# Four conditioning chunks behind the layer branch, and two combinings behind the last activation

## The chip, the core and the metric

The kernel runs on one core of a Trainium2 chip. The metric is device time in microseconds (us), from the program's start to its end. The engines are TensorE (PE: matmuls; PEld: its weight loads), VectorE (DVE), ScalarE (ACT), GpSimd (POOL) and SyncE (SP), which here only issues transfers; 16 DMA engines move data. Matmul results go to PSUM, everything else on the chip lies in SBUF.

## What is computed

A two-layer network over 256 latent tokens and 256 context tokens, 1024 features wide, batch 1. Of the reference, what matters here:

```python
for l in range(DEPTH):                       # DEPTH = 2
    mod = jax.nn.silu(c) @ w_ada[l] + b_ada[l]          # 6 vectors of 1024
    mod_c = jax.nn.silu(c_ctx) @ w_ada[l] + b_ada[l]
    x, xc = trunk_layer(x, xc, mod, mod_c, ..., need_ctx_out=(l < DEPTH - 1))
return rms_norm(x, norm_f)

def trunk_layer(...):
    sh1, sc1, g1, sh2, sc2, g2 = jnp.split(mod[:, None, :], 6, axis=-1)
    x = x + g1 * token_mixer(modulate(rms_norm(x, norm1), sh1, sc1), ...)
    x = x + g2 * moe_ffn(modulate(rms_norm(x, norm2), sh2, sc2), ...)   # 16 experts, top 2 of one group
```

Conditioning vector number 3 of a layer is sh2, the shift ahead of the experts. The token mixer has two attentions, a Fourier and a pooling branch, each gated. An expert computes silu(x w1) * (x w3) and multiplies the product with w2.

## The kernel before, in words

**Products.** Weights are f32 in HBM. A chunk of 1 MB (128 x 2048 f32) is loaded to a stage buffer and split into two f16 tiles: ScalarE writes whi, VectorE the remainder wlo (lines 319 and 323, `split`). A product is then three f16 matmuls: whi x high, whi x low, wlo x high (L580 to L582, `mm3`). Conditioning chunks (kind "ada") and the w2 chunks of the last expert (WHOLE) are exceptions: they are "raw", multiplied in f32 straight from the stage buffer.

**The weight stream.** `Stream` holds the order of all chunks, found by a dry run of the same program. `get` takes the next chunk and lets `fill` issue loads on SP as far as buffers are free (four, NSTG, in the mixer). A buffer of a split chunk is free after its split, that of a raw chunk after its matmuls. `tick` asks for one more split ahead, within `look` chunks. The stream of layer 2 (`Wn`) is made and filled with its first four loads inside the last steps of layer 1 (`batch`), behind a VectorE memset.

**The branch.** Behind the experts of each layer stands a branch (`tc.If`, L1511) for a second round of experts that these inputs don't need. All engines meet there: none starts on layer 2 before the last one has come.

**Conditioning.** `ada(l, which)` makes one vector in four chunks: 8 x 2 f32 matmuls with 32 columns (L500) give sums in PSUM, `split` turns them into adah and adal, and `second` turns those into columns (L477, L478; small VectorE instructions L481, L488). It is a generator; in layer 2 `ada(1, 3)` is the list SIDE1 and is advanced by `with_side` at every third step of the filling work in the first attention. Its chunks stand in the weight stream where the dry run asks for them.

**Start of layer 2.** `norm_steps`: four diagonal tiles from the norms (L555), then per feature block k matmuls with x (L568) into one of four PSUM tiles "mm", ScalarE's h (L572), VectorE's hH and hL (L573, L574). `W.tick(ahead)` asks for the first splits before the blocks. `project` takes the keys' and values' chunk first.

**The end.** The last expert (e = 15) runs w1, then w3 (`up`), then `hidden`: ScalarE's Silu and VectorE's product sa (L1382, L1383), then `down` with raw w2 (L1312). Experts 0 to 13 have put their results in DRAM; these are gathered per token tile t and rank (POOL, L1399). `combine(t, True)` scales and adds the gathered rows: L1406 on ScalarE, L1407, L1409, L1410 on VectorE. Experts 14 and 15 reach the tokens through a matmul with the transposed one-hot matrix (`back`, L1333, tiles acc), whose results `add` joins to x (yl L1340, then L1345). yHL is the split of `down`'s result. The output is normed and stored.

**Order on the engines.** Tile's scheduler orders each engine's instructions by a model of their readiness. `keep_in_program_order` pins an instruction behind the one that was traced before it on the same engine; what is traced later may still be put ahead of either. An engine then takes its queue in that order.

## Time and profile before

| | |
|---|---|
| median of three runs | 1454.68 us (1453.69 to 1455.19) |
| the profiled execution's own time | 1449.04 us |
| its span, first to last instruction | 1447.30 us |
| mean granted TensorE clock | 0.984 of full |
| TensorE busy | 1345.9 us, 93% |
| VectorE busy | 1118.3 us, 77% |
| ScalarE busy | 952.8 us, 66% |
| DMA | 383.31 MB, mean 265 GB/s |

The profile is of one execution; its times count from the span's start. A busy TensorE is not TensorE at its peak, and a share over the whole span mixes stages with different limits. A wait is read with the engine and line that ended it.

### The profile page before, as it was taken

Reading aid. Unit: us, or ns where it says so; the run is one execution under the profiler, and the core shown is the slowest. Engines: PE = TensorE matmul, PEld = TensorE weight load, DVE = VectorE, ACT = ScalarE, POOL = GpSimd, SP = SyncE. Lnnn points to the kernel's source line nnn. Section 1 sums busy time; section 2 is a strip of 40 time slices with the busy share of each in tenths; the row PEclk is TensorE's granted clock in tenths of the full one; section 3 lists DMA queues with packets and bytes.
Section 4 is the critical chain, followed back from the end, with each engine's and each line's share of the span. In section 5 each row is a group of like instructions: output and inputs, shape, how many; then the busy total and the mean of one; then the engine's idle time right before and its main releaser. Section 6 shows DMA issues by size and latency. Waiting matters only on the chain. (4 is left out here: it accounts for less than half of the span.)

```text
span 1447.3 us, 33640 instructions
## 1 busy us (share of the span) xinstructions
PE 1345.9 (93%) x14151; PEld 923.4 (64%) x14151; DVE 1118.3 (77%) x2003; ACT 952.8 (66%) x1431; POOL 16.5 (1%) x16
## 2 busy tenths in 40 slices
PE   5999999999999998999999978899999989999994
PEld 3545445444444586777777746577788767777771
DVE  3888647786554557898988889878977888989995
ACT  3777535665433347889888656856855569899981
POOL 0000000000000000000000010000000000000010
PEclk9999999999999999999999999999999999999997
DMA  9559772678794336789999564783999679999981
GB/s 365 216 132 222 217 232 88 175 219 228 238 364 159 131 101 250 293 344 420 395 419 380 222 253 163 200 240 103 238 310 364 239 280 342 420 420 418 405 327 63
DMA packets 146416, 383.31 MB, mean 265 GB/s; under 512 B 91856, under 2 KB 93904, under 8 KB 108112
## 3 DMA queue, kind: packets, MB, share of 16 engines
q1 hardware_dynamic: 133136, 355.24, 69.5%
q10 hardware_dynamic: 11392, 19.56, 3.6%
q0 software_dynamic: 1728, 6.29, 1.3%
q8 instruction: 112, 1.84, 0.5%
q14 instruction: 48, 0.39, 0.1%
HBM read 344.88 MB, written 15.20 MB: 249 GB/s over the span
## 5 line engine op out<-in xcount | busy, mean ns | idle before, releaser
L323 DVE SCALAR_TENSOR_TENSOR wlo<-stage,whi 128x1024 f16<-128x1024 f32 (+1 forms) x212 | 318.5, 1522 | 104.0 <-ACT whi L319 103.6
L582 PE MATMUL mm<-hH,wlo 128*128 128x96 f16 (+2 forms) x1824 | 395.5, 260 | 1.0 <-DVE wlo L323 1.0
L580 PE MATMUL mm<-hH,whi 128*128 128x96 f16 (+2 forms) x1824 | 395.3, 260 | 0.7 <-DVE gate L992 0.7
L581 PE MATMUL mm<-hL,whi 128*128 128x96 f16 (+2 forms) x1824 | 395.3, 260 | 0.0
L319 ACT ACTIVATE whi<-stage 128x1024 f16<-128x1024 f32 (+1 forms) x212 | 269.6, 1294 | 126.3 <-PE mm L581 86.7
L582 PEld LDWEIGHTS <-wlo 128*128 128x128 f16 x3104 | 304.0, 98 | 72.7 <-DVE wlo L323 2.7
L580 PEld LDWEIGHTS <-whi 128*128 128x128 f16 x3104 | 303.9, 98 | 71.6 <-issue 3.4
L581 PEld LDWEIGHTS <-whi 128*128 128x128 f16 x3104 | 303.9, 98 | 71.2 <-issue 1.2
L323 DVE SCALAR_TENSOR_TENSOR wlo<-ext,whi 128x2048 f16<-128x2048 f32 x116 | 262.1, 2286 | 42.6 <-ACT whi L319 42.6
L319 ACT ACTIVATE whi<-ext 128x2048 f16<-128x2048 f32 x116 | 217.8, 1904 | 9.4 <-PE mm L582 7.4
L581 PE MATMUL mm<-xg,whi 128*128 128x96 f16 x1024 | 132.3, 206 | 0.0
L582 PE MATMUL mm<-xg,wlo 128*128 128x96 f16 x1024 | 132.3, 206 | 0.0
L580 PE MATMUL mm<-xg,whi 128*128 128x96 f16 x1024 | 132.3, 206 | 0.0
L581 PE MATMUL py<-wlo,hd 128*96 128x512 f16 x240 | 90.9, 379 | 8.9 <-DVE wlo L323 8.7
L582 PE MATMUL py<-whi,hd 128*96 128x512 f16 x240 | 90.2, 381 | 6.8 <-DVE hd L321 6.0
L580 PE MATMUL py<-whi,hd 128*96 128x512 f16 x240 | 91.0, 379 | 0.0
L580 PE MATMUL mm<-brH,whi 128*128 128x512 f16 (+1 forms) x256 | 83.5, 326 | 0.0
L582 PE MATMUL mm<-brH,wlo 128*128 128x512 f16 (+1 forms) x256 | 83.4, 326 | 0.0
L581 PE MATMUL mm<-brL,whi 128*128 128x512 f16 (+1 forms) x256 | 83.4, 326 | 0.0
L1264 PE MATMUL mm<-Dg,merged 128*128 128x384 f16 x384 | 71.0, 338 | 3.8 <-DVE Dg L1197 1.8
L500 PE MATMUL mm<-stage,cpad 128*32 128x256 f32 x768 | 58.1, 406 | 13.3 <-DMA stage<-in_w_ada_dram 13.2
L825 DVE SCALAR_TENSOR_TENSOR P<-E,rl,P 128x512 f16<-128x512 f32 (+1 forms) x96 | 59.2, 658 | 9.7 <-ACT P L824 9.5
(313 smaller groups left out, 2050.3 us busy)
## 6 DMA issues: line engine op xcount, KB each, us to landing
ext<-in_w_dram SPq DMA_DIRECT2D x118, 1024.0 KB, 9.0
stage<-in_w_dram SPq DMA_DIRECT2D x62, 1024.0 KB, 9.0
stage<-in_w_ada_dram SPq DMA_DIRECT2D x48, 1024.0 KB, 6.3
stage<-in_w_gate_dram SPq DMA_DIRECT2D x32, 1024.0 KB, 5.8
stage<-in_w_in_dram SPq DMA_DIRECT2D x16, 1024.0 KB, 6.9
stage<-in_w_branch_dram SPq DMA_DIRECT2D x32, 512.0 KB, 4.6
ydram<-ys ACTq DMA_DIRECT2D x56, 192.0 KB, 7.1
stage<-in_w_out_dram SPq DMA_DIRECT2D x8, 1024.0 KB, 5.5
```

The source lines that it names most:

```text
L319: a = nc.scalar.activation(hi, src, AF.Copy, scale=scale)
L323: b = nc.vector.scalar_tensor_tensor(lo, src, scale, hi, op0=ALU.mult, op1=ALU.subtract)
L500: pe.matmul(ps[32 * j:32 * j + 32, :], self.cpad[:, 2 * k:2 * k + 32], st[:, k, :], start=k < 4, stop=k >= 4, tile_position=(0, 32 * j))
L580: pe.matmul(ps, wH(k), xH(k), start=first and k == 0, stop=False)
L581: pe.matmul(ps, wH(k), xL(k), start=False, stop=False)
L582: pe.matmul(ps, wL(k), xH(k), start=False, stop=last and k == nk - 1)
L825: dve.scalar_tensor_tensor(pv[:, 1, qt, :], E[qt][:, 0:nk], r[:, qt:qt + 1], pv[:, 0, qt, :], op0=ALU.mult, op1=ALU.subtract)
L1264: pe.matmul(ps[:, 0:SLOTS], h2[n][t][:, cs(k)], Dg[:, t].rearrange("p e c -> p (e c)"), start=t == 0, stop=t == ntt - 1)
```

## The change

At the start of layer 2 `ada_sums` takes the four chunks of vector 3 and multiplies them at once, two chunks to one PSUM tile "adas" (tag pst, two such tiles). Splitting and the small matmuls follow behind the norm (`run_all(first)` in `mixer`). SIDE1 is gone, so nothing of it is left in the attention, nor its four ticks. In the stream of layer 2 these chunks now come first, so the four loads issued ahead are theirs. At the end, `combine(0)` moves from ahead of the last w3 to behind `hidden`, where `combine(1)` stands; sa of the last expert is pinned behind what VectorE was given before, and the first VectorE instruction of each combining is pinned behind what was traced before it, which for the first is sa. ScalarE's scaling was pinned already; for t = 0 that is now behind the last Silu.

```diff
@@ -101,7 +101,6 @@
 
 
 SIDE0 = ((0, 2), (0, 4), (0, 3), (1, 1), (1, 0), (1, 2), (1, 4))
-SIDE1 = ((1, 3),)
 GAP = (2, 2)
 BACK = 3
 HX = (9, 10)
@@ -459,7 +458,25 @@
             dve.scalar_tensor_tensor(dst if it == 2 else y, t, 1.5, y, op0=ALU.add, op1=ALU.mult)
 
 
-    def ada(self, l, which, tick=True):
+    def ada_sums(self, l, which):
+
+        W, out = self.W, []
+        for c in range(4):
+            st = W.get("ada", "w_ada", (l,), which * D + c * 256)
+            if c % 2 == 0:
+                bank = self.ps.tile([128, 512], F32, "adas", tag="pst")
+            ps = bank[:, c % 2 * 256:c % 2 * 256 + 256]
+            self.ada_products(ps, st)
+            out.append(ps)
+        return out
+
+    def ada_products(self, ps, st):
+        for k in range(KD):
+            j = k % 4
+            self.nc.tensor.matmul(ps[32 * j:32 * j + 32, :], self.cpad[:, 2 * k:2 * k + 32], st[:, k, :], start=k < 4, stop=k >= 4,
+                                  tile_position=(0, 32 * j))
+
+    def ada(self, l, which, tick=True, sums=None):
         nc, const, W = self.nc, self.const, self.W
         pe, dve = nc.tensor, nc.vector
         gate = which % 3 == 2
@@ -493,14 +510,14 @@
 
         prev = None
         for c in range(4):
-            st = W.get("ada", "w_ada", (l,), which * D + c * 256)
-            ps = self.mm((128, 256))
-            for k in range(KD):
-                j = k % 4
-                pe.matmul(ps[32 * j:32 * j + 32, :], self.cpad[:, 2 * k:2 * k + 32], st[:, k, :], start=k < 4, stop=k >= 4,
-                          tile_position=(0, 32 * j))
-            if tick:
-                W.tick()
+            if sums:
+                ps = sums[c]
+            else:
+                st = W.get("ada", "w_ada", (l,), which * D + c * 256)
+                ps = self.mm((128, 256))
+                self.ada_products(ps, st)
+                if tick:
+                    W.tick()
             if prev:
                 second(*prev)
             ph = self.wk.tile([128, 256], F16, "adah", tag="t2")
@@ -604,20 +621,23 @@
             side = chain(*(self.ada(*x) for x in SIDE0))
         else:
             self.W = self.Wn
-            side = chain(*(self.ada(*x) for x in SIDE1))
+            first = self.ada(l, 3, False, self.ada_sums(l, 3))
+            side = None
         with ExitStack() as scope:
             self.lay = Pool(scope.enter_context(self.tc.tile_pool(name=f"lay{l}", bufs=1)), {})
             self.late = self.ada(l, 5, False)
-            self.mixer(l, nq, side)
+            self.mixer(l, nq, side, None if full else first)
             self.moe(l, nq, side)
 
-    def mixer(self, l, nq, side):
+    def mixer(self, l, nq, side, first=None):
         nc, tc, A, W, wk, sm = self.nc, self.tc, self.A, self.W, self.wk, self.sm
         pe, act, dve = nc.tensor, nc.scalar, nc.vector
         C, LC, split, mm3 = self.C, self.LC, self.split, self.mm3
         full = nq == NTOK
         nst = nq // T
         hH, hL = self.h if full else self.norm_mod(l, 1, NTOK, 0, 2)
+        if first:
+            run_all(first)
         scope = ExitStack()
         at = Pool(scope.enter_context(tc.tile_pool(name=f"att{l}", bufs=1)),
                   {"pmH": 4, "pmL": 4, "a2": 3, "P": 3, "pt": 2 - full, "E": 3, "G": 2})
@@ -1066,7 +1086,7 @@
                 dve.scalar_tensor_tensor(y, ps, DS, g1[:, t // 2, :], op0=ALU.mult, op1=ALU.mult)
                 dve.tensor_tensor(self.xt(t)[:, s5], self.xt(t)[:, s5], y, op=ALU.add)
                 self.x_stat(t, c, c * 256, 256)
-        run_all(side)
+        run_all(side or ())
         for _ in range(GAP[0]):
             next(self.late, None)
 
@@ -1380,7 +1400,9 @@
             def hidden(e, pa, pb):
                 sa = wk.tile([128, 4, CAP], F32, "sa", tag="t2")
                 act.activation(sa, pa, AF.Silu, scale=DS)
-                dve.scalar_tensor_tensor(sa, pb, AS * DS, sa, op0=ALU.mult, op1=ALU.mult)
+                last = dve.scalar_tensor_tensor(sa, pb, AS * DS, sa, op0=ALU.mult, op1=ALU.mult)
+                if pe_all and e == NE - 1:
+                    tc.keep_in_program_order(last)
                 if e in whole:
                     return sa
                 hd = [wk.tile([128, 4, CAP], F16, f"hd{i}", tag="t2") for i in range(2)]
@@ -1404,8 +1426,9 @@
             def combine(t, gated=False):
                 y0, y1 = mid["yg", t]
                 tc.keep_in_program_order(act.activation(y0, y0, AF.Copy, scale=wr[:, 0, t:t + 1]))
-                dve.scalar_tensor_tensor(y0, y1, wr[:, 1, t:t + 1], y0, op0=ALU.mult, op1=ALU.add)
+                both = dve.scalar_tensor_tensor(y0, y1, wr[:, 1, t:t + 1], y0, op0=ALU.mult, op1=ALU.add)
                 if gated:
+                    tc.keep_in_program_order(both)
                     TT(y0, y0, mid["g2"][t // 2], op=ALU.mult)
                     TT(xt(t), xt(t), y0, op=ALU.add)
 
@@ -1449,8 +1472,6 @@
                     next(more, None)
                 if prev is not None:
                     down(e - 1, prev)
-                if e == NE - 1 and pe_all:
-                    combine(0, True)
                 if e == NE - 1 and not pe_all:
                     fetch()
                     dw = mid["dw"] = wk.tile([128, 4, 128], F32, "dw", tag="t2")
@@ -1472,6 +1493,7 @@
                     accumulate(e - 1)
                 prev = hidden(e, pa, pb)
                 if e == NE - 1 and pe_all:
+                    combine(0, True)
                     combine(1, True)
                 if e == 1:
                     index()
```

## Rows read from the trace of the kernel before

**Rows 1.** Timeline, TensorE, the end: start us, us, instruction, idle before, releaser

```profile
1412.78 0.21 PE L582 MATMUL mm<-hH,wlo 128*128 128x96 f16 x1
...
1413.98 0.29 PE L1294 MATMUL hotT<-id,Dg 128*96 128x128 f16 x2
1420.31 8.25 PE L1312 MATMUL py<-stage,sa 128*96 128x512 f32 x12 [6.04 <-DVE sa L1383]
```

**Rows 2.** Timeline, VectorE, the end

```profile
1414.24 1.28 DVE L1407 SCALAR_TENSOR_TENSOR yg<-yg,wr 128x1024 f32<-128x1024 f32 x1 [2.86 <-DMA yg<-ydram,late]
...
1418.57 1.22 DVE L1409 TENSOR_TENSOR yg<-yg,merged 128x1024 f32<-128x1024 f32 x1
1419.70 0.55 DVE L1383 SCALAR_TENSOR_TENSOR sa<-mm,sa 128x384 f32<-128x384 f32 x1
1420.17 1.22 DVE L1410 TENSOR_TENSOR X<-X,yg 128x1024 f32<-128x1024 f32 x1
...
1427.60 0.75 DVE L323 SCALAR_TENSOR_TENSOR yHL<-py,slotw,yHL 96x512 f16<-96x512 f32 x1 [3.75 <-ACT yHL L319]
1429.03 0.69 DVE L1340 SCALAR_TENSOR_TENSOR yl<-acc,merged 128x512 f32<-128x512 f32 x1 [0.69 <-PE acc L1333]
```

**Rows 3.** Timeline, all engines, behind the branch between the layers

```profile
857.18 1.06 ACT L319 ACTIVATE whi<-stage 128x1024 f16<-128x1024 f32 x1 [3.79 <-DVEq L1511]
...
858.40 9.53 PE L568 MATMUL mm<-diag,X 128*128 128x128 f32 x64 [7.56 <-DVE diag L555]
...
870.31 0.69 DVE L574 TENSOR_TENSOR hL<-h,hH 128x512 f16<-128x512 f32 x1
...
872.72 0.38 PE L582 MATMUL mm<-hH,wlo 128*128 128x512 f16 x1
```

**Rows 4.** Groups, 857 to 872: busy us, mean ns, idle before

```profile
L574 DVE TENSOR_TENSOR hL<-h,hH 128x512 f16<-128x512 f32 x8 | 5.3, 688 | 0.1
L323 DVE SCALAR_TENSOR_TENSOR wlo<-stage,whi 128x1024 f16<-128x1024 f32 x4 | 4.8, 1219 | 0.0
L573 DVE CAST hH<-h 128x512 f16<-128x512 f32 x8 | 3.3, 422 | 0.5 <-ACT h L572 0.5
```

**Rows 5.** Timeline, TensorE: a conditioning chunk at the program's start and in the attention

```profile
8.98 1.94 PE L500 MATMUL mm<-stage,cpad 128*32 128x256 f32 x16 [8.98 <-DMA stage<-in_w_ada_dram]
...
901.70 1.07 PE L500 MATMUL mm<-stage,cpad 128*32 128x256 f32 x16
```

**Rows 6.** Windows: us, busy of PE, PEld, DVE, ACT, POOL, clock, DMA, GB/s

```profile
862.00:863.00 1.00, 1.00 (x7) 1.00 (x7) 0.96 (x3) 1.00 (x3) 0.00 (x0) 0.55 0.98 131
863.00:864.00 1.00, 1.00 (x12) 1.00 (x11) 1.00 (x2) 0.87 (x2) 0.00 (x0) 1.00 0.95 393
```

**Rows 7.** DMA issues, 840 to 1010: count, size, median us to landing

```profile
stage<-in_w_in_dram SPq DMA_DIRECT2D x8, 1024.0 KB, 6.7
...
stage<-in_w_ada_dram SPq DMA_DIRECT2D x4, 1024.0 KB, 4.9
```

**Rows 8.** Groups, 902 to 932

```profile
L500 PE MATMUL mm<-stage,cpad 128*32 128x256 f32 x64 | 4.3, 386 | 0.0
...
L319 ACT ACTIVATE adah<-mm 128x256 f16<-128x256 f32 x4 | 1.6, 390 | 0.0
```

**Rows 9.** Windows of 10 us, first attention of layer 2

```profile
910.00:920.00 10.00, 7.75 (x88) 4.58 (x85) 9.73 (x28) 10.00 (x22) 0.00 (x0) 1.00 0.63 173
```

**Rows 10.** Timeline, ScalarE, first attention of layer 2

```profile
921.30 1.06 ACT L319 ACTIVATE whi<-stage 128x1024 f16<-128x1024 f32 x1 [1.26 <-DMA stage<-in_w_gate_dram]
```

**Rows 11.** Windows of 2 us, first attention of layer 2

```profile
926.00:928.00 2.00, 2.00 (x17) 0.55 (x18) 1.02 (x3) 1.54 (x3) 0.00 (x0) 0.56 1.13 212
```

**Rows 12.** Timeline, ScalarE, the end

```profile
1402.97 0.49 ACT L1382 ACTIVATE sa<-mm 128x384 f32<-128x384 f32 x1
...
1406.16 1.90 ACT L319 ACTIVATE whi<-X 128x2048 f16<-128x2048 f32 x1
...
1415.43 1.15 ACT L1406 ACTIVATE yg<-yg,wr 128x1024 f32<-128x1024 f32 x1 [4.45 <-DMA yg<-ydram,late]
```


## Prediction, made before the result was known

> **What bounds the kernel now.** The page's busy times say that TensorE is busy nearly throughout, but that is a mean over stages. So I went on to two stretches that the change touches: the last 47 us, and the stretch behind the branch between the layers.
>
> *The end.* In TensorE's timeline the last w3 product starts at 1412.78 and lasts 0.21, so the inputs of sa are complete at 1413.0. The first product of the last expert with its down weights (L1312) starts only at 1420.31, and the row says why: 6.04 us without work, ended by VectorE's sa [rows 1]. VectorE's timeline shows where sa was: it starts at 1419.70, behind three instructions of the combining, of which the first alone waited 2.86 for gathered rows [rows 2]. The second L1407 stands just ahead of L1409, so it started 1.28 before 1418.57, at 1417.3, when the last gather was in. The end is set by a queue order with DMA latency inside it.
>
> *Behind the branch.* ScalarE is let go at 857.18; TensorE's first work is L568, which turns x into features, at 858.40. VectorE splits each feature block into hH and hL, and the first projection needs all eight: the last hL ends at 870.31 + 0.69 = 871.0, the projection's last product starts at 872.72 [rows 3]. In the groups of this stretch VectorE spends 0.69 + 0.42 on a block and 1.22 on a weight split [rows 4]: eight blocks and four splits fill 13.8 of the 15 us. I take VectorE as the bound here. The weights are in place: ScalarE's first act is to split one of the four chunks loaded ahead.
>
> **The end, worked out.** The change pins sa ahead of both combinings. VectorE is idle from 1414.24 - 2.86 = 1411.4 on, so sa runs at 1413.0 to 1413.6 (0.55). TensorE has small products until 1413.98 + 0.29 = 1414.3; L1312 starts there, 6.0 earlier [rows 1, 2].
>
> That isn't the gain yet, as VectorE must still combine. Its first instruction starts when its gather is in, as before at 1414.24. L1407, L1409 and L1410, twice, are 2 x (1.28 + 1.22 + 1.22) = 7.4, less about 0.08 of overlap at each of five joints: 7.0. With 0.2 allowed for two small slot weights they end at 1421.4; the second L1407 comes to its turn at 1417.8, after its gather. Then yHL (0.75) and 0.7 for TensorE's acc (from yHL's end at 1428.35 to yl): yl starts at 1422.8 instead of 1429.03 [rows 2]: 6.2. TensorE doesn't set this: even at the old rate of 12 L1312 in 8.25 us [rows 1], the first eight are done at 1414.3 + 5.5 = 1419.8. From yl on the chain is as before. I take **-6.2**. Bounds: -7.5 if yHL slips in ahead of one last combining instruction (1.22 sooner); the other end is in the rivals.
>
> **The conditioning, worked out.** Four chunks move, each with a 1 MB load, 16 matmuls, one adah (ScalarE), one adal (VectorE), four small matmuls and two small VectorE instructions.
>
> *Where they arrive.* TensorE is let go about when ScalarE is, 857.2. A chunk takes 1.94 us at the slow rate, as at the start of the program, and 1.07 at the full one [rows 5]. The granted clock was still 0.55 from 862 to 863 and 1.00 after, with matmuls running since 858.40 [rows 6]; with matmuls from 857.2 I let it rise at 861.8. Two chunks are done at 861.1, four at 863.6. L568 then starts 5.2 later than it did, but at the full rate, 12 matmuls per us [rows 6]: the first eight give ScalarE a block at 864.7, and VectorE gets it at 865.7.
>
> The weights are the other half. What is loaded ahead is now conditioning; the projection's first load can be issued only when the first chunk has been multiplied, at 859.2, and lands 4.9 later, as those four loads did [rows 7], at 864.1. Its two splits, with which the stretch began [rows 3], now fall among the blocks. VectorE: 865.7 + 8 x 1.06 + 2 x 1.22 = 876.6 for the last hL, 5.6 later. The projection's last product follows by 0.7, at 877.3, against 872.72: 4.6 later. The conditioning's own VectorE work runs mostly in the wait before 865.7; I allow 0.5 for its tail. Together **+5.1**. Bounds: +1.0 if TensorE alone counted (64 matmuls at 12 per us end at 868.9; they ended at 867.9), and +6.9 if the load took 6.7, as the w_in loads did [rows 7].
>
> No row shows a writer and a reader on one PSUM bank: each chunk has had its own, and here two share one. The Trainium skill's page "PSUM — Partial Sum Buffer" (section "PSUM bank collisions raise a hardware error") says that two engines' accesses to one bank and quadrant must be kept apart. By that rule the first chunk's split waits for the second's matmuls, two adal would reach the blocks, and the sum would be about 0.8 higher. I keep the sum without it.
>
> *Where they left.* They were multiplied in the first attention, from 902 on. TensorE loses 4.3 us of matmuls there, ScalarE 1.6 of adah [rows 8]. But from 910 to 920 TensorE is busy for only 7.75 of 10 us and ScalarE for all 10 [rows 9], so the matmuls filled idle time, and I count ScalarE's 1.6. And the conditioning held buffers of the weight stream: ScalarE waited 1.26 for a gate load at 921.30 [rows 10]. With the buffers free earlier this wait goes; late next is VectorE's part of the same softmax. Together **-2.9**. Bounds: 0 (softmax and transposes hide it) and -7.2 (TensorE's share too).
>
> Edits at nothing: the conditioning's ticks go, four requests for splits ahead; the projections still make two per gate chunk, and if that weren't enough, four splits of 1.22 would come late. The loads change places on SP's queue, where the next transfer behind them is not needed for many microseconds; POOL has no part in it.
>
> **Sum.** 5.1 - 2.9 - 6.2 = -4.0 us. The profiled execution took 1449.04 (span 1447.30), 5.6 less than the median of the three runs, 1454.68. 1445.0 there is **1450.7** in the median. A measurement of this kernel can tell about 0.2%, 2.9 us, from no change: faster is below 1451.8, slower above 1457.6.
>
> **Rivals.** *Nothing comes back in the attention:* TensorE has idle time there, and a shorter queue may only wait longer. 5.1 - 6.2 = -1.1: 1453.6, no change.
>
> *All of it comes back:* if the queue order on TensorE delays the scores, 5.1 - 7.2 - 6.2 = -8.3: 1446.4. Against it: the idle time in rows 9.
>
> *The clock falls in the attention.* From 926 to 928 the granted clock was 0.56 [rows 11]. Without the conditioning's matmuls the gaps get wider; four more microseconds at half rate cost 2.0: 1452.7, no change. The Trainium skill's page "TensorE: Matmul & The Clock Gate" (section "HAM oscillation") speaks against this change in the same way: repeated waits between short bursts let the clock drop.
>
> *Slower: the scalings stall ScalarE.* The two scalings of gathered rows (L1406) are now pinned behind the last Silu alone, which ran at 1402.97, ahead of two weight splits, the later one at 1406.16 [rows 12]. If both come before these splits, ScalarE waits for the gather of 1415.43, is done at 1416.6, and the splits (1.90 each) at 1420.4. VectorE's 2.28 and 2.3 of products put sa's end at 1425.6, and with combining, yHL and acc behind it yl comes at 1434, 5.0 later than it did. With +2.2 from the conditioning: +7.2, 1461.9. It decides from the point where a scaling stands before the split at 1406.16. So far they were pinned behind yHL; nothing in the trace shows how the order falls now.
>
> *sa is late all the same:* +2.2, 1456.9, no change. Against it: the pins name just these instructions.
>
> **Chances.** Forecast 0.47; nothing back 0.20; all back 0.14; clock 0.08; stalled scalings 0.07; sa still late 0.04. The forecast's margin to 1451.8 is 1.1, its terms are uncertain by about 2, so three quarters of it are faster: 0.35, with 0.14 and 0.06 from the spread of two others 0.55. Slower 0.07, no change 0.38. The range runs from just below "all back" to between "nothing back" and "sa late": 1445.5 to 1455.5; the forecast's own is 1447.7 to 1453.7.
>
> **What would show it.** Right: L1312 starts under 1 us after TensorE's last small product, and the time from the last w3 product to yl falls from 16 to about 10; 64 conditioning matmuls start at about 857, the first w_in load goes out at about 859, the last hL comes 5 to 6 later; no wait for the gate load in the attention. Wrong: a last hL less than 3 later (VectorE wasn't the bound), an attention shorter by more than 5 or by nothing, or L1406 ahead of a weight split.

## The result and the profile after

| | before | after |
|---|---|---|
| median of six runs each | 1453.78 us (1449.52 to 1455.19) | 1461.51 us (1457.75 to 1465.36) |
| the profiled execution's own time | 1449.04 us | 1461.74 us |
| its span | 1447.30 us | 1460.0 us |
| mean granted TensorE clock | 0.984 | 0.982 |
| TensorE, VectorE, ScalarE busy | 93, 77, 66% | 93, 77, 65% |

The change made the kernel slower: the ratio is 1.0059 (95% interval 1.0037 to 1.0081), 7.7 us in the medians. The forecast was 4.0 us faster; its range ended 6 us below the result.

The page shows none of it: the busy shares are the same within 1%. The two timelines laid side by side do. Up to the branch both kernels issue the same instructions in the same order on TensorE, VectorE and ScalarE, and yet the profiled execution after is already 4.2 us late there. That part of the 12.7 us between the two profiles is the spread of executions, not the change (cond_only, an experiment with the same new start of layer 2, stands at -0.1 there), so every comparison below is taken from the branch on: the start of an instruction, less its start before, less the same difference for VectorE's reciprocal root (the row at 855.17 before). "Shift" means this from here on. (q, k and v are the queries, keys and values of the attention; their squares give the norms.)

| instruction, its start before | change | cond_only | cond_late | cond_split |
|---|---|---|---|---|
| third q's squares, ScalarE, 896.67 | +10.5 | +10.1 | +8.3 | +2.5 |
| sums of the q's, VectorE, 902.00 | +13.7 | +13.4 | +11.5 | +5.8 |
| first exponential, ScalarE, 907.76 | +15.1 | +14.7 | +12.1 | +6.0 |
| v of the second projection, ScalarE, 981.40 | +13.3 | +13.0 | +9.2 | +4.5 |
| last expert's yHL, ScalarE, 1405.57 | +10.9 | +13.1 | +6.7 | +3.8 |
| last norm, VectorE, 1438.15 | +8.1 | +13.1 | +6.4 | +3.4 |

(The other columns are experiments.) How far can a shift be trusted? end_only, an experiment that issues what before issues up to the last expert, has -0.2 in the first three rows, +0.4 in the fourth and +3.8 at the last expert's yHL. So a shift is good to about 0.6 us as far as the second projection, and behind it one execution can be off by 4 us.

In the change 10.5 us are lost before the third q, 3.3 more up to the sums of the q's, the attention and what follows give about as much back, and the end gains 2.8 of the 6.2 forecast.

**Behind the branch.** TensorE's timeline after (start us, us, instruction, idle before and its releaser):

```profile
857.97 2.80 PE L476 MATMUL adas<-stage,cpad 128*32 128x256 f32 x48 [2.94 <-ACTq L1533]
861.15 1.07 PE L476 MATMUL adas<-stage,cpad 128*32 128x256 f32 x16 [0.39 <-SPq L1533]
862.58 4.70 PE L585 MATMUL mm<-diag,X 128*128 128x128 f32 x40 [0.36 <-DVE diag L572]
...
869.29 4.38 PE L585 MATMUL mm<-diag,X 128*128 128x128 f32 x24 [2.01 <-ACT h L589]
...
875.11 0.18 PE L494 MATMUL mm<-sel,adah 128*128 128x2 f16 x1 [1.44 <-ACT adah L318]
876.29 0.18 PE L495 MATMUL mm<-sel,adal 128*128 128x2 f16 x1 [1.00 <-DVE adal L322]
...
880.55 0.59 PE L597 MATMUL mm<-hH,whi 128*128 128x512 f16 x1
...
887.36 0.38 PE L599 MATMUL mm<-hH,wlo 128*128 128x512 f16 x1
```

The first thing to see is favourable: TensorE starts at 857.97, while VectorE is at the norm ahead of the branch until 860.1 (L458 below). (So it is not true of this branch that no engine starts on layer 2 before the last one has come.) It runs three chunks in 2.80 us and the fourth in 1.07, the full rate of [rows 5], so they are through at 862.2, before the diagonal tiles are there. L585 (L568 before) starts no later. What follows stood in the forecast with 0.5 us: from 875.11 to 880.51 TensorE takes the small matmuls of the conditioning in groups of one or three, behind seven waits for adah or adal, 5.6 us together, and the first projection (L597) cannot pass them. Its last product starts at 887.36 against 872.72 [rows 3], a shift of 10.5. ScalarE and VectorE show why the small matmuls are late:

```profile
866.33 2.00 ACT L318 ACTIVATE whi<-stage 128x1024 f16<-128x1024 f32 x2 [1.50 <-DMA stage<-in_w_in_dram]
...
874.68 0.38 ACT L318 ACTIVATE adah<-adas 128x256 f16<-128x256 f32 x1
...
880.07 0.38 ACT L318 ACTIVATE adah<-adas 128x256 f16<-128x256 f32 x1 [0.68 <-DVE ada L505]
```

```profile
859.94 0.16 DVE L458 SCALAR_TENSOR_TENSOR rnorm<-rs_t,rs_y 128x1 f32<-128x1 f32 x1
...
876.15 0.68 DVE L591 TENSOR_TENSOR hL<-h,hH 128x512 f16<-128x512 f32 x1
...
881.16 0.42 DVE L322 SCALAR_TENSOR_TENSOR adal<-adas,adah 128x256 f16<-128x256 f32 x1
```

On ScalarE the first adah stands behind all the feature blocks, and weight splits stand between it and the others; on VectorE the adal stand beside and behind the last hL, again with weight splits (1.22 us each) between them. The later load of the first projection's weights costs less: its split stands on ScalarE ahead of most feature blocks and waits 1.50 (866.33), TensorE then waits 2.01 for h (869.29), and the last hL ends at 876.8, only 1.7 later against the branch than before [rows 3]. The last adal ends at 881.6. And while TensorE waits, its granted clock falls to half (0.50 from 880.5 to 884.0), so that the products that do run take 0.63 instead of 0.38 us. Window from 874 to 884 (us; busy of TensorE, its loads, VectorE, ScalarE, GpSimd; granted clock; DMA share; GB/s):

```profile
874.00:884.00 10.00, 4.74 (x24) 2.05 (x25) 9.14 (x25) 5.77 (x10) 0.00 (x0) 0.67 0.78 302
```

**In the attention.** TensorE's waits between 885 and 925 (total, times, longest), after and before:

```profile
PE pq L695 <- ACT sqh L318: 5.6, 2, 4.9
```

```profile
PE pq L675 <- ACT sqh L319: 2.4, 2, 1.6
```

The last of the q's sums waits 3.3 us longer for ScalarE. From the branch to the first exponential VectorE runs 13 splits from stage buffers in the change; before it ran 10.

**At the end.** ScalarE, VectorE and TensorE after:

```profile
1420.62 0.68 ACT L318 ACTIVATE yHL<-py,slotw 96x512 f16<-96x512 f32 x1 [0.32 <-PE py L599]
1424.82 1.15 ACT L1428 ACTIVATE yg<-yg,wr 128x1024 f32<-128x1024 f32 x1 [3.52 <-DMA yg<-ydram,late]
1425.87 1.89 ACT L318 ACTIVATE whi<-X 128x2048 f16<-128x2048 f32 x1
```

```profile
1427.80 2.29 DVE L322 SCALAR_TENSOR_TENSOR wlo<-X,whi 128x2048 f16<-128x2048 f32 x1 [4.22 <-ACT whi L318]
...
1433.89 0.56 DVE L1403 SCALAR_TENSOR_TENSOR sa<-mm,sa 128x384 f32<-128x384 f32 x1 [3.14 <-PE mm L599]
...
1439.27 0.74 DVE L322 SCALAR_TENSOR_TENSOR yHL<-py,slotw,yHL 96x512 f16<-96x512 f32 x1
...
1441.06 0.68 DVE L1360 SCALAR_TENSOR_TENSOR yl<-acc,merged 128x512 f32<-128x512 f32 x1
```

```profile
1433.57 0.28 PE L599 MATMUL mm<-hH,wlo 128*128 128x96 f16 x1
...
1434.65 0.29 PE L1314 MATMUL hotT<-id,Dg 128*96 128x128 f16 x2
1434.78 5.34 PE L1332 MATMUL py<-stage,sa 128*96 128x512 f32 x12
```

The first scaling (L1428) stands on ScalarE ahead of the split of X and waits 3.52 for its gathered rows. The split starts at 1425.87; yHL ahead of it ended at 1421.3, and before the change the split started with no idle time ahead of it [rows 12]. So VectorE's remainder waits 4.22, w3's last product starts at 1433.57 and sa at 1433.89. Behind sa all goes as the forecast had it, and better: TensorE's L1332 follows its last small product at once, yHL slips in ahead of two combining instructions, and yl starts 7.5 us behind the last w3 product, where it took 16 before [rows 1, 2].

### The profile page after: what moved, and what is told of

Read it like the earlier page. It is cut to its first block, busy times and chain, and to the rows that moved or that the text cites. A ratio compares the mean times of both kernels' runs of the same rounds, so it can differ in the third digit from the quotient of the medians.

```text
span 1460.0 us, 33653 instructions
## 1 busy us (share of the span) xinstructions
PE 1351.3 (93%) x14151; PEld 925.7 (63%) x14151; DVE 1118.7 (77%) x2003; ACT 953.7 (65%) x1431; POOL 14.9 (1%) x16
## 5 line engine op out<-in xcount | busy, mean ns | idle before, releaser
L597 PE MATMUL mm<-hH,whi 128*128 128x96 f16 (+2 forms) x1824 | 399.0, 262 | 3.2 <-ACT whi L318 2.5
L597 PEld LDWEIGHTS <-whi 128*128 128x128 f16 x3104 | 304.8, 98 | 75.1 <-issue 5.1
L318 ACT ACTIVATE whi<-ext 128x2048 f16<-128x2048 f32 x116 | 217.8, 1904 | 10.1 <-PE mm L599 7.4
L597 PE MATMUL mm<-xg,whi 128*128 128x96 f16 x1024 | 132.3, 206 | 0.0
L597 PE MATMUL py<-whi,hd 128*96 128x512 f16 x240 | 91.0, 379 | 0.0
L597 PE MATMUL mm<-brH,whi 128*128 128x512 f16 (+1 forms) x256 | 83.5, 326 | 0.0
L817 DVE TENSOR_REDUCE mx<-S 128x1 f32<-128x512 f32 (+1 forms) x96 | 56.4, 595 | 12.3 <-PE S L816 12.0
```

What stands on the lines that cost most here:

```text
L318: a = nc.scalar.activation(hi, src, AF.Copy, scale=scale)
L597: pe.matmul(ps, wH(k), xH(k), start=first and k == 0, stop=False)
L817: dve.tensor_reduce(mx[:, qt:qt + 1], S, axis=AX.X, op=ALU.max)
```

## The experiments

Theory from the two profiles: the small matmuls in TensorE's queue behind the branch, and the scaling ahead of the split at the end. Rivals: the weights, which are no longer loaded ahead; the end as the main loss; a delay in layer 1.

### The two parts, and what each would be without its new wait

cond_only is the change without its edits to the end. end_only is the reverse. cond_late is cond_only with the conditioning's follow-up moved:

```diff
-        if first:
-            run_all(first)
...
             W.tick()
+            if first and glob:
+                run_all(first)
             vH = at.tile([128, 4, 128], F16, "vH")
```

end_fix is end_only with the first scaling issued ahead of the last w3 again (scale(t) holds the line that is taken out of combine):

```diff
-                tc.keep_in_program_order(act.activation(y0, y0, AF.Copy, scale=wr[:, 0, t:t + 1]))
+                if not gated or t:
+                    scale(t)
...
+                if e == NE - 1 and pe_all:
+                    scale(0)
```

> The change's first part alone; the end is as before. Theory (the loss is made behind the branch, where the small matmuls of the conditioning stand in TensorE's queue ahead of the first projection and wait for adah and adal): about 10 us slower than before (the change's +7.7 in the medians plus the 2.4 that its end gave back in the trace), with the small matmuls done only 24 to 25 us after the branch. Rival (the loss is made at the end, by the scaling that waits on ScalarE): 1 to 2 us slower at most. Rival (most of the loss is layer 1's, which the change does not touch): within 3 us of before.

> The change's second part alone; the conditioning is as before. Theory: the first scaling again stands on ScalarE ahead of a weight split and waits about 3.5 us for its gather, so that only 2 to 3 us of the 6.2 forecast come: about -2.4 us. Rival (the end is where the change loses): 3 us or more slower. If the scaling does not stand ahead of the split here, -6.

> The change's first part alone, as cond_only, but the splits and small matmuls of the conditioning are written behind the products of keys and values, so that TensorE goes from the feature blocks straight to the first projection. Theory (the small matmuls in the queue cost 8 to 9 us): about +2 us against before, and 8 us less than cond_only. Rival (the projection's weights come late because the four loads ahead are now conditioning): still +8 to +10, with the first projection waiting for a weight split instead. A wait on TensorE for wlo or a DMA ahead of the first projection would show it.

> The change's second part alone, with one thing put back: ScalarE's scaling of the first token tile is issued where it was before the change, ahead of the last w3. Theory (the scaling ahead of the weight split undid the end's gain): the split runs at once, sa is no longer late, and the end gains what the forecast gave it: about -6 us, 3 to 4 better than end_only. Rival (sa is late for another reason, the last w3 or the weight split itself): no better than end_only.

| | median us | before, same chip | ratio, 95% interval |
|---|---|---|---|
| cond_only | 1464.10 | 1450.27 | 1.0102 (1.0073 to 1.0131) |
| end_only | 1449.64 | 1450.27 | 0.9989 (0.9975 to 1.0004) |
| cond_late | 1461.17 | 1450.27 | 1.0066 (1.0041 to 1.0090) |
| end_fix | 1443.86 | 1450.27 | 0.9957 (0.9938 to 0.9976) |

The loss is the conditioning's, all of it: +13.8 in the medians of cond_only, where about 10 were expected, and no loss in end_only. Layer 1 is no part of it (cond_only stands at -0.1 at the branch). The end's two versions differ by one place in ScalarE's queue. ScalarE in end_only, then in end_fix:

```profile
1413.27 0.68 ACT L319 ACTIVATE yHL<-py,slotw 96x512 f16<-96x512 f32 x1 [0.32 <-PE py L582]
1417.58 1.15 ACT L1408 ACTIVATE yg<-yg,wr 128x1024 f32<-128x1024 f32 x1 [3.63 <-DMA yg<-ydram,late]
1418.63 1.89 ACT L319 ACTIVATE whi<-X 128x2048 f16<-128x2048 f32 x1
```

```profile
1408.89 0.68 ACT L319 ACTIVATE yHL<-py,slotw 96x512 f16<-96x512 f32 x1 [0.32 <-PE py L582]
1409.47 1.90 ACT L319 ACTIVATE whi<-X 128x2048 f16<-128x2048 f32 x1
...
1413.02 1.15 ACT L1408 ACTIVATE yg<-yg,wr 128x1024 f32<-128x1024 f32 x1 [0.73 <-DMA yg<-ydram,late]
```

In end_only the split of X starts 4.7 us behind yHL's end (1413.95), in end_fix it follows it. VectorE in end_fix:

```profile
1416.56 0.56 DVE L1383 SCALAR_TENSOR_TENSOR sa<-mm,sa 128x384 f32<-128x384 f32 x1 [1.85 <-PE mm L582]
...
1422.04 0.74 DVE L323 SCALAR_TENSOR_TENSOR yHL<-py,slotw,yHL 96x512 f16<-96x512 f32 x1
```

The shift from the last expert's yHL to the last norm is -2.7 in end_only (+3.8 to +1.1) and -8.5 in end_fix (+0.4 to -8.0). In the medians end_fix gains 6.4. So the stalled scaling is shown, and end_fix beats both kernels.

cond_late missed its theory: its time, +9.6 by the ratio, is the rival's (+8 to +10), though not for the rival's reason. Against cond_only it saves 5.2 us by the ratios (0.0036 x 1450) and 2.9 by the medians, not 8, and the two intervals overlap. TensorE goes straight to the projection, without a wait for weights, but the small matmuls stop it later, between v and the first q:

```profile
870.86 0.38 PE L597 MATMUL mm<-hH,whi 128*128 128x512 f16 x1
...
882.69 0.18 PE L495 MATMUL mm<-sel,adal 128*128 128x2 f16 x1 [1.12 <-DVE adal L322]
...
886.43 0.19 PE L495 MATMUL mm<-sel,adal 128*128 128x2 f16 x1 [1.30 <-DVE adal L322]
```

So moving the follow-up by some lines was the wrong cure; it has to come off the path of TensorE's queue and off ScalarE's and VectorE's busy stretch at once.

### Splitting early, multiplying late, and holding other splits back

cond_split splits the sums at once into tiles of their own, while ScalarE and VectorE wait for the first block, and leaves the small matmuls to the attention's filling steps. late_hold and split_hold are cond_late and cond_split with the gate and branch splits of the first filling steps pinned behind what was written before them. both_fixed is split_hold with end_fix's end.

```diff
+            cols = [[at.tile([128, 256], F16, f"ada{i}{c}") for i in range(2)] for c in range(4)]
+            for pair_, ps in zip(cols, first):
+                split(*pair_, ps, AS)
+            side = self.ada(l, 3, False, cols)
+        hH, hL = self.h if full else self.norm_mod(l, 1, NTOK, 0, 2)
```

```diff
+        self.kn.pin, pin = self.kn.pin or self.kn.hold and spec[1] != "w_in", self.kn.pin
         self.kn.split(hi[:, s], lo[:, s], st[:, s], WS)
```

> As cond_late, and the splits of gate and branch weights that the first filling steps of the attention ask for are pinned behind the work written before them (three of them, 1.22 us each on VectorE, stood ahead of the first softmax in the change and in cond_late, where before the change none of them had run). Theory (these three early splits are the second cost behind the branch): the first softmax comes 3 to 4 us earlier against the branch than in cond_late, and of that 2 to 4 us are left at the end: +5 to +8 against before. Rival (the delay is only the small matmuls of the conditioning): no better than cond_late.

> The change's first part alone, but the conditioning's sums are split as soon as they are multiplied, into tiles of their own, while ScalarE and VectorE wait for the first feature block, and the small matmuls are advanced in the first attention, at every third filling step, as before the change. Theory (waits of TensorE for adah and adal cost 4 to 5 us in cond_late and more in cond_only): the projection starts at once and k comes at most 2 us later against the branch than before; the three early weight splits stay, so +3 to +6 in all, 4 to 5 less than cond_late. Rival (the weights loaded late set the start): still +8 or more.

> As cond_split, and with the gate and branch splits pinned as in late_hold. Theory (these two costs are all that the conditioning's arrival adds): within 2 us of before, from -2 to +2. Rival (the attention gives back what it no longer has to do, 2.9 as forecast or more): -3 or better. Rival (a third cost): +4 or more.

> split_hold for the conditioning and end_fix for the end together. Theory: the two parts do not touch each other, so the sum of both: -5 to -8 against before, about what end_fix alone gives. Rival (the conditioning pays once its own costs are gone): -9 or better.

| | median us | before, same chip | ratio, 95% interval |
|---|---|---|---|
| late_hold | 1462.79 | 1452.40 | 1.0067 (1.0042 to 1.0093) |
| cond_split | 1455.20 | 1452.40 | 1.0015 (0.9999 to 1.0030) |
| split_hold | 1457.30 | 1452.40 | 1.0025 (1.0007 to 1.0043) |
| both_fixed | 1449.77 | 1452.40 | 0.9983 (0.9964 to 1.0002) |

cond_split shows the size of the follow-up: TensorE goes from the blocks to the projection, and the shift at the third q is +2.5 instead of the +10.1 of cond_only. The ratio falls with it from 1.0102 to 1.0015, more than expected and with intervals far apart: where the follow-up stands is worth 11 us in the medians, 13 by the ratios.

```profile
871.00 5.48 PE L591 MATMUL mm<-diag,X 128*128 128x128 f32 x32 [2.59 <-ACT h L595]
876.32 0.38 PE L603 MATMUL mm<-hH,whi 128*128 128x512 f16 x1
```

The pins were a miss: late_hold is 9.7 us slower than before by its ratio (5 to 8 were expected), split_hold 3.6 (within 2). They did what they say: the step from the third q to the sums of the q's fell from 3.3 to 1.3 (late_hold +8.6 to +9.8, split_hold +2.5 to +3.8), with 11 splits ahead of the softmax instead of 13. But at the first exponential nothing was left of it (split_hold +6.2, cond_split +6.0), and at the second projection it was +8.8 against +4.5. The theory of the three splits fell as a cause that can be cured by holding them back. both_fixed gains 2.5 by its ratio, where 5 to 8 were expected and end_fix alone gained 6.2 (these two intervals overlap).

### Only the departure

Five runs time the departure alone; what each leaves out stands with its expectation. no_cond takes the four chunks away altogether; loads_only leaves their places and loads; places_only the places alone; read1 leaves the loads and one product of each chunk, as the code writes it; read16 writes 16 products and no splits. The vector is set to zero in all five, so they time what is left and do not compute the network.

```diff
+        for c in range(4):
+            st = self.W.get("ada", "w_ada", (l,), which * D + c * 256)
+            ps = self.mm((128, 256))
+            for k in range(1):
...
+            self.W.tick()
+            yield
```

cond_fill is cond_split with 16 written products of constants at each of the four steps; split_places is cond_split with the four places kept as empty ones.

In reading them, count the matmuls in the traces. An f32 product that the code writes is two matmuls there: a chunk has 8 written products and 16 matmuls, the four chunks 64 [rows 8]. So read1 leaves 8 matmuls of 64, and read16 has 128, not the 64 that its expectation takes for granted; cond_fill puts in 128 where 64 were taken away.

> The kernel before without the four conditioning chunks of vector 3 of layer 2: their loads, products, splits and small matmuls are left out and the vector is set to zero, so that nothing is moved and only the departure from the first attention is timed. Theory (their products kept TensorE's granted clock up between the scores; in the change, cond_split and cond_late the attention shows 13 to 17 us at about half clock where before shows 4): the attention again has 10 us or more at half clock, and the kernel comes 2 to 5 us slower than before in spite of having less to do. Rival (forecast: ScalarE and the gate load become free): 2.9 faster. Rival (hidden work): within 1.

> As cond_split, with 16 products of constants (32 columns of conditioning input, 256 columns of constants, f32, results not read) put in at each of the four steps where a conditioning chunk stood before the change. Theory (the clock falls for want of these products): the half clock in the attention goes back to 6 us or less, and the kernel is 3 to 5 us faster than cond_split, within 2 of before. Rival (the clock falls because the softmax is late for another reason): still 13 us or more at half clock, no better than cond_split or up to 4.3 us slower, which is what the products take.

> As no_cond (products, splits and small matmuls of vector 3 of layer 2 left out, the vector set to zero), but its four chunks keep their places in the weight stream and are loaded as before; nobody reads them. Theory (no_cond is slower because without these places three splits of gate and branch weights are asked for and run ahead of the first softmax): the first softmax comes as early as before the change, and the kernel is 0 to 3 us faster than before, at least 3 faster than no_cond. Rival (the products kept TensorE's clock up, and that was worth the time): still 2 to 5 us slower than before, with 10 us or more at half clock.

> As loads_only, with the four places kept in the order of the stream and their buffers taken, but nothing loaded into them. Theory (order and buffers decide, not the transfers): within 1.5 us of loads_only. Rival (the four loads themselves delayed others): 1 to 3 us faster than loads_only.

> As cond_split (the change's first part with early splits), and the four places that the chunks had in the stream of the attention are kept as empty ones, with a buffer and nothing loaded. Theory (arrival behind the branch costs 2.5 and the rest of cond_split's loss is the early splits): the first softmax comes 2 to 3 us later than before instead of 5.9, and at the end 0 to +2.5 against before. Rival (order of the stream does not matter): +2.8 as cond_split.

> As loads_only, but one product of each chunk (32 columns of conditioning input, 256 columns of weights) stays at its place in the attention, so that its stage buffer is held until then, as before the change; the other 15 products, the splits and small matmuls are left out. loads_only showed the three early splits although the places were kept; there nothing held the buffers. Theory (held buffers keep the gate and branch weights from being there in time to be split ahead of the softmax): the last q's sums wait 1.6 us for ScalarE instead of 4.9, the first softmax starts as before the change, and the kernel is level with before or up to 3 us faster, 3 or more faster than loads_only. Rival (the 60 products that are missing kept TensorE's clock up, and that is what the time went for): +2 to +4 as loads_only, although the softmax starts in time.

> As read1, with all 16 products of each chunk at their places: only the splits, the small matmuls and the two small VectorE instructions of the conditioning are left out. Theory: order and clock are those of before, so level with before or up to 1.5 us faster. Rival of read1 (the clock): if read1 is slower and this one is not, the clock is worth the difference.

| | median us | before, same chip | ratio, 95% interval | shift at 896.67, 902.00, 907.76, 981.40, 1405.57 |
|---|---|---|---|---|
| no_cond | 1455.07 | 1451.68 | 1.0024 (1.0011 to 1.0038) | 0.0, +3.2, +4.6, +6.0, +3.8 |
| loads_only | 1455.33 | 1452.69 | 1.0025 (1.0010 to 1.0040) | 0.0, +3.3, +4.7, +5.7, +4.0 |
| places_only | 1456.21 | 1452.69 | 1.0034 (1.0020 to 1.0048) | +0.5, +3.7, +4.5, +5.3, +3.0 |
| read1 | 1453.40 | 1452.29 | 1.0013 (0.9994 to 1.0031) | -0.1, -0.1, 0.0, +1.6, +0.7 |
| read16 | 1452.25 | 1452.29 | 1.0000 (0.9984 to 1.0016) | -0.1, -0.1, -1.0, +1.5, +0.2 |
| cond_fill | 1454.51 | 1451.68 | 1.0020 (1.0005 to 1.0034) | +2.5, +5.7, +5.9, +6.4, +3.8 |
| split_places | 1452.66 | 1452.69 | 1.0003 (0.9991 to 1.0016) | +1.3, +4.6, +5.5, +2.3, +4.4 |

no_cond has less to do and is slower. Up to the third q it runs as before to 0.1 us; then three weight splits of gate and branch stand on VectorE between the steps that rotate the q's (tiles ropes):

```profile
898.88 1.22 DVE L323 SCALAR_TENSOR_TENSOR wlo<-stage,whi 128x1024 f16<-128x1024 f32 x1
...
900.71 1.21 DVE L323 SCALAR_TENSOR_TENSOR wlo<-stage,whi 128x1024 f16<-128x1024 f32 x1
...
902.51 1.22 DVE L323 SCALAR_TENSOR_TENSOR wlo<-stage,whi 128x1024 f16<-128x1024 f32 x1
```

Before, the first gate load went out at 902.83, too late for that. Its issue on SP's queue, before, then in loads_only, then in read1:

```profile
902.83 0.33 SPq L219 DMA_DIRECT2D stage<-in_w_gate_dram  x1
```

```profile
885.12 0.33 SPq L219 DMA_DIRECT2D stage<-in_w_gate_dram  x1
```

```profile
906.06 0.33 SPq L219 DMA_DIRECT2D stage<-in_w_gate_dram  x1
```

A place in the stream that nobody reads gives its buffer back at once, so in loads_only the gate load goes out at 885.12 and there are 13 splits ahead of the softmax; one product per chunk, at its old place, holds the buffer, and there are 10 again. TensorE's wait for the last q's squares goes with it, loads_only and read1:

```profile
PE pq L684 <- ACT sqh L319: 5.6, 2, 4.9
```

```profile
PE pq L689 <- ACT sqh L319: 2.4, 2, 1.6
```

So the forecast's term "With the buffers free earlier this wait goes" was real, with the wrong sign: the loads it sets free bring filling work forward, and the order of the queues puts that ahead of the softmax. The traces show this order cleanly. What it costs is less sure: read1 is 1.7 us faster than loads_only by the ratios, where 3 or more were expected, and the two intervals overlap.

The clock was the other candidate. Windows of 90 us over the first attention, each shifted with its kernel: before, after, no_cond, cond_split, cond_fill, read1.

```profile
890.00:980.00 90.00, 81.35 (x838) 59.90 (x837) 70.73 (x169) 59.69 (x116) 0.00 (x0) 0.98 0.70 194
```

```profile
905.00:995.00 90.00, 78.83 (x710) 56.99 (x709) 68.81 (x156) 58.70 (x112) 0.00 (x0) 0.92 0.59 151
```

```profile
893.00:983.00 90.00, 75.80 (x667) 54.24 (x666) 67.78 (x152) 57.63 (x111) 0.00 (x0) 0.92 0.55 142
```

```profile
900.00:990.00 90.00, 79.81 (x751) 59.10 (x749) 68.85 (x160) 58.50 (x112) 0.00 (x0) 0.91 0.57 150
```

```profile
892.00:982.00 90.00, 82.58 (x841) 58.85 (x838) 69.39 (x163) 59.35 (x112) 0.00 (x0) 0.98 0.55 148
```

```profile
894.00:984.00 90.00, 77.53 (x739) 57.35 (x737) 68.35 (x156) 58.25 (x112) 0.00 (x0) 0.98 0.71 193
```

Products can keep the clock up: cond_fill, which differs from cond_split by its constants alone, has 0.98 against 0.91. It is no faster (1.0020 and 1.0015). But this does not price the clock, as the constants take 10.0 us of TensorE in the window (below), where the 64 matmuls taken away had taken 4.3 [rows 8]; they could hide a gain.

```profile
892.00:982.00 90.00, 9.99 (x128) 3.90 (x128) 0.98 0.55 148
```

The shifts say a little more. From the first exponential to v of the second projection cond_split gets 1.5 us back at 0.91 and the change 1.8 at 0.92, while no_cond loses 1.4 at 0.92 and read1 1.6 at 0.98: the time of this stretch does not follow the clock. read1 keeps 0.98 with 8 matmuls instead of 64; there the softmax is in time. What the fall costs by itself stays open.

split_places is level with before in the median, with the early splits still in it (+3.3 from the third q to the sums) and a first exponential 5.5 late, where 2 to 3 were expected. Its profile is 4.4 late in the last expert after being 1.0 late at 1022, a step like that of end_only, where nothing was changed; so where its median comes from stays open.

### The clock behind the branch

end_fix_warm and end_fix_warm32 put 64 and 32 written products of constants where the change has its chunks, on top of end_fix. In the traces these are 128 and 64 matmuls; the change has 64:

```diff
+            self.idle_products(64, "pst")
```

> As end_fix (conditioning as before the change), with 64 products of constants behind the branch, where the change multiplied its four chunks; results not read. TensorE is let go there before VectorE has the diagonal tiles, and in the change its clock stayed full through these products. Theory (L568 then runs at the full clock and starts no later, and nothing of the weight stream is moved): the first feature block comes 0.9 earlier and the first projection 1 to 3 us earlier than in end_fix, so -7 to -9 against before. Rival (VectorE's 13.8 us of splits set this stage): no better than end_fix, -5 to -7.

> As end_fix_warm with half as many products behind the branch; there 64 lasted 7.11 us and held L568 up until 861.17. Theory (32 last 3.6 us and end before the diagonal tiles are there, so that L568 runs at the full clock from its old start): the first projection 1 to 2 us earlier than in end_fix, -7 to -8 against before. Rival (VectorE's splits set this stage): as end_fix, -6.

end_fix_warm: 1445.58 us, 0.9959 (0.9942 to 0.9976), as end_fix. end_fix_warm32: 1451.48 us, 0.9991 (0.9977 to 1.0005), worse than end_fix. TensorE and ScalarE in end_fix_warm:

```profile
854.13 7.11 PE L466 MATMUL idle<-cst,cpad 128*32 128x256 f32 x128 [2.94 <-ACTq L1528]
861.17 5.07 PE L575 MATMUL mm<-diag,X 128*128 128x128 f32 x43
```

```profile
858.48 4.83 ACT L319 ACTIVATE whi<-stage 128x1024 f16<-128x1024 f32 x5
863.21 7.37 ACT L579 ACTIVATE h<-mm,ada,ada 128x256 f32<-128x256 f32 x16
```

This tells nothing of the clock's worth: with the products in, the order on ScalarE changed, five pieces of weight splits run in one go ahead of the first block, which comes 2.3 later in both, and in end_fix_warm32 the first attention loses another 7 us. There the granted clock is 0.92 from 894 to 984, with the conditioning as before: in this run the lower clock and a loss go together, and nothing tells which is the cause. A test that adds instructions also tests the new order.

## Why the prediction was wrong

The forecast's three terms, by the shifts in the change's profile:

| term | forecast | measured |
|---|---|---|
| conditioning arriving | +5.1 (+1.0 to +6.9) | +10.5 |
| attention, give-back | -2.9 (-7.2 to 0) | +0.4 (+10.5 to +10.9, with the work after it; +3.0 in cond_only) |
| the end | -6.2 (to -7.5) | -2.8 |
| sum | -4.0 | +8.1 (7.7 in the medians) |

**Where they arrive: "the conditioning's own VectorE work runs mostly in the wait before 865.7; I allow 0.5 for its tail".** This is the step that failed. The tail took 8.8 us: the shift of the last hL is 1.7 and that of the projection's last product 10.5. Between them lie TensorE's seven waits and the products at half clock. I had costed the adal as busy time on VectorE and had not asked what stands behind the small matmuls on TensorE, nor where adah stands on ScalarE. cond_split, which takes both off the path, shows 2.5 for the whole arrival.

**The same step's other half was too dear.** TensorE was to run the chunks at the slow clock from 857.2; it had full rate and was through before VectorE's tiles. The first w_in load was to be issued at 859.2; less the 4.2 of layer 1 it went out at 857.3. The last hL came 1.7 later, not 5.6. The text named this sign ("a last hL less than 3 later (VectorE wasn't the bound)"), and it came. The profile before could have told: TensorE waits once between 857 and 873, for the diagonal tiles, and from 858.40 on runs through to the projection's end. All waits of TensorE in this stretch, before:

```profile
PE mm L568 <- DVE diag L555: 7.6, 1, 7.6
```

Nor does a row give the 0.7 from the last hL to the projection's last product; rows 3 have 872.72 - 871.0 = 1.7, and with that the sum for the arrival is 6.1.

**PSUM banks.** The 0.8 that the sum would get by the rule of the Trainium skill's page "PSUM — Partial Sum Buffer" (section "PSUM bank collisions raise a hardware error") was kept out; no run here separates it.

**Where they left: -2.9.** ScalarE's 1.6 and the wait for the gate load were counted as gains. no_cond, the departure alone, has its first exponential 4.6 late and is +0.24% in the median. (read16 is level, but with twice the products.) Of the rivals "nothing comes back" was the nearest, but no rival had a net loss here. The edit costed at nothing held the hint: "if that weren't enough, four splits of 1.22 would come late". They came early, three of them. The size of this term is not known well: +0.4 in the change and +3.0 in cond_only, with the 4 us of one execution in both.

**The clock falls in the attention.** It did, by more than priced: a mean of 0.92 over 90 us is 7.2 us of full clock lost, against 1.8 before. The Trainium skill's page "TensorE: Matmul & The Clock Gate" (section "HAM oscillation") is right here in that the clock falls; whether the fall costs the time, no run here separates.

**The end: -6.2.** The mechanism was right, and the size was short: end_fix gains 8.5 in its profile, beyond the bound of 7.5, as yHL slips in ahead of two instructions instead of one, and 6.4 in the medians. The change itself got 2.8, by the rival with the stalled scalings, at whose decision point ("a scaling stands before the split at 1406.16") one scaling stands. It was priced for both scalings ahead of both splits, at 11 us against the forecast; one ahead of one costs 4.6 at the split, and the yl is earlier than before, not later. I gave it 0.07 because nothing showed the order; an open order deserved more. That its time, 1461.9, is next to the measured 1461.5 is luck: it put the loss at the end, which gained, and had +2.2 for the conditioning, which lost it all.

**Median and profile.** Layer 1, where nothing changed, differs by up to 7.5 us between the profiles (cond_fill -1.3, cond_split +6.2). Only shifts from the branch could carry the argument, and behind the second projection not even these to better than 4 us.

## What to carry to other kernels

Price a moved step by its followers: list what each of its small products waits for, and what stands behind that product in its engine's queue. A buffer that is freed earlier is not a gain by itself; ask which load it lets go, and where the work that the load makes ready will stand in the queues. And when an instruction with a long DMA wait is pinned, look for the work on the same engine that the pin lets it overtake.

## What the runs showed of the hardware that was not expected

- TensorE left the branch before VectorE had finished the norm and ran 48 f32 matmuls in 2.80 us after 2.94 us of idle time, at a granted clock of 1.00, where L568 after 7.56 us of idle time ran at 0.50 to 0.55 until 863 [rows 3, 6].
- An f32 product that the code writes is two matmuls in the trace: 64 written products of constants in end_fix_warm are 128 matmuls, 7.11 us.
- Eight small matmuls at the right places (read1), with the softmax in time, went with a mean granted clock of 0.98 over the attention, 128 matmuls of constants in four groups (cond_fill), with the softmax late, as well; no_cond and cond_split, with neither, had 0.92 and 0.91.
- From the first exponential to the second projection the time did not follow this clock: cond_split got 1.5 us back at 0.91, read1 lost 1.6 at 0.98.
